# Up projection of a streaming encoder step: state stores issued by GpSimd, filters nine steps behind, another order of the first group's blocks

## The chip, the cores and the metric

The kernel runs on one core of a Trainium2 chip, and its time is the device time in microseconds of one execution. The engines named here are TensorE (PE; its weight loads are shown as PEld), VectorE (DVE), ScalarE (ACT), GpSimd (POOL) and SyncE (SP). DMAs are issued from the queues of SP, ACT and POOL.

## The reference

One layer of a hybrid encoder for 256 frames of a new stream and 16 new frames of each of 8 running streams, 384 rows in all, in float32. What matters here is the feed-forward part at the end:

```python
h2 = rmsnorm(x, norm_ffn_g)
up = h2 @ w_up                                   # (384, 2048) @ (2048, 11264)
g_half, u_half = up[..., :D_FF], up[..., D_FF:]  # D_FF = 5632
ext_f = concatenate([ffn_buf, g_half], axis=1)   # the state: the last 2 rows before
gc = causal_dwconv(ext_f, ffn_dw_w, ffn_dw_b)    # 3 taps along time
x = x + (silu(gc) * u_half) @ w_down
new_ffn = ext_f[:, -2:]                          # the state that is stored
```

Ahead of it come the norm and one combined input projection, a conformer convolution branch, forgetting attention, and the projections that join them.

## The kernel before

**Products in three parts.** A float32 product is made of three matmuls on rounded parts. Each operand is split into a high half (`hi`, a cast on ScalarE, L155) and a low half (`lo`, a subtraction on VectorE, L156), and hi*hi, hi*lo and lo*hi are added up in one PSUM bank (L1158 to L1160 in the up projection, L305 to L307 in the others).

**Weights.** They come in tiles of 256 rows x 512 columns (512 KB, `raw`, L138), issued from SP. In the feed-forward part five buffers rotate for `raw` and three for each of `hi` and `lo`. `plan` is the list of the weight tiles in the order of their use; `ahead` fetches and splits them ahead of the matmuls, with a raised priority (SPLIT_AHEAD).

**Order of the work.** TensorE's order is the program's. On the other engines, and in the queues, a planner orders the instructions at build time by priority and by its own estimate of when each can start; buffers are handed out there too. Each engine then runs its list strictly in that order. `high_priority(offset=...)` moves an instruction ahead of others in the planner's list.

**The up projection.** The 5632 columns of each half are done in 11 groups of 512 (`up_group`). In `FFN_PLAN` group 0 is followed by group 1, and then two groups alternate with one down projection: 0, 1, 2, down(0, 1), 3, 4, down(2, 3), ... 9, 10, down(8, 9, 10). So groups 2, 4, 6, 8 and 10 follow another group at once, and 3, 5, 7 and 9 follow a down projection. The 2048 rows of K are four panels of 512 (`q` = 0 to 3). Panels 0 and 1 (`MIXED`) use a fast 2x2 scheme (steps `b22`, `t3`, `t1` for the u half, `b11`, `t2`, `b21`, `t4` for the g half) that saves products by adding weight tiles on VectorE first: L200 and L205 (steps t3 and t1) and L209 (steps t2 and t4, into `sums`). Panels 2 and 3 (`PLAIN`) are done plainly, in two K blocks each: `pu0`, `pu1` for the u half and `pg0`, `pg1` for the g half. A group has 92 products of three matmuls: 4 in each of b22, t3, b11 and b21, 2 in each of t1, t2 and t4, 6 in each plain step. `phases` gives the order of the steps: in all groups but the first the plain steps are spread between the others; in the first group (`first`) they stand behind the others of the same half, so that the plain operand `xg` of panel 3, which is made last (L1050 and L1051), is wanted late. `run` walks through one half, and is called twice a group.

**Banks and evacuations.** There are five PSUM banks `acc` and three `misc`. The u half uses five `acc` banks (p5, p7, q3, q2, tu), the g half p1, tg and q6 in `misc` and p2 and q4 in `acc`. Evacuations: p5 L1195 and L1196, p7 L1199, q3 L1202, q2 L1205, the samples' rows L1208, p1 L1211 and L1212, q6 L1216 and L1219, p2 L1223, q4 L1226. Most go into row tiles u and g of the pool `block`, which has four buffers. In the first group this pool also holds the transpose of the old FFN state (L1076 to L1080).

**From rows to columns.** The rows of u and of g are transposed in 32x32 blocks on VectorE (L319), written to DRAM by four DMAs of GpSimd's queue (`turn`, L324) and read back by a fifth (L329), which completes the transpose.

**The filter.** `up_g_done` stores the state rows of a group (L1098 once, L1100 twice, 4 KB and 16 KB each) and queues the convolution with `after(n, fn)`: `fn` is emitted n + 1 steps of the `tick` counter later, a step being three products (nine matmuls). `fill` copies the columns into `extf` (ScalarE L1107; GpSimd L1110 to L1114 for the rows that overlap), `taps(m)` makes the three taps and the SiLU (L1127 to L1130), `product(m)` multiplies by u and splits the result for the down projection (L1135 to L1139), for m = 0 to 3.

Of the kernel before, what the change touches and what calls it, by code (L numbers as in the profile page):

```python
# [11 lines left out]
ALU = mybir.AluOpType  # L12
# [22 lines left out]
MIXED = (0, 1)  # L35
# [6 lines left out]
def hybrid_step(  # L42
# [121 lines left out]
    def planned(w, k0, cols, nk, *more):  # L164
        for k in range(k0, k0 + nk, 2):
            for cl in (cols,) + more:
                plan.append([rows_of(w, k, c, n) for c, n in cl])
# [3 lines left out]

    def phases(first):
        def spread(steps, plain):
            if first:
                return steps + plain
            n, m = len(steps), len(plain)
            out = []
            for i, st in enumerate(steps):
                out.append(st)
                out += plain[i * m // n:(i + 1) * m // n]  # L180
            return out

        up = [(what, q) for q in MIXED for what in ("b22", "t3", "t1")]
        gate = [(what, q) for q in MIXED for what in ("b11", "t2")] + [(what, q) for q in MIXED for what in ("b21", "t4")]
        return [spread(up, [(f"pu{h}", q) for q in PLAIN for h in range(2)]),
                spread(gate, [(f"pg{h}", q) for q in PLAIN for h in range(2)])]

    def planned_mixed(w, c1, c2, first):
        held = {}

        def add(fn):
            plan.append(lambda: split(fn(), 512))
# [15 lines left out]
        def grown(q, name):  # L208
# [5 lines left out]
                "b21": lambda q: single("b21", 4 * q + 2, c1), "t4": lambda q: grown(q, "b21")}  # L214
        for steps in phases(first):
            for what, q in steps:
                if what[0] == "p":
                    planned(w, 4 * q + 2 * int(what[2]), [({"u": c2, "g": c1}[what[1]], 512)], 2)
                else:
                    add(lambda what=what, q=q: make[what](q))  # L220

# [34 lines left out]
    def after(units, fn):  # L256
        later.append([units, fn])
# [836 lines left out]
    def up_g_done(g, box):  # L1094
        def done():
            cs = slice(512 * g, 512 * (g + 1))
            rows = box[0].rows
            nc.sync.dma_start(prompt_ffn[0, 0, :, cs], rows[126:128, 1, :])  # L1098
            for r in range(2):
                nc.sync.dma_start(sample_ffn[0, :, r, cs], rows[14 + r::16, 2, :])  # L1100
            gd = box[0].moved().rearrange("p i t q c -> p (i t) q c")

            def fill():
                for m in range(4):
# [9 lines left out]
                    nc.gpsimd.tensor_copy(e5[:, 0, 1, 0, 0:2], e5[:, 3, 0, 1, 16:18])  # L1114
            after(7, fill)

# [15 lines left out]
            def product(m):  # L1132
# [6 lines left out]
                tt(lo, av, f(hi), op=ALU.subtract)  # L1139
            pace = 1 if g == 10 else 2  # L1140
            for m in range(4):
                after(8 + pace * m, lambda m=m: taps(m))
                after(9 + pace * m + pace, lambda m=m: product(m))
        return done
# [24 lines left out]
    def up_group(g):  # L1169
# [34 lines left out]
        def q2(ps):  # L1204
            stt(rows("u")[:, 1], ps, scale[1], e1, op0=ALU.mult, op1=ALU.subtract)  # L1205

# [23 lines left out]

        def products(steps):
            return [plain(q, int(what[2]), *({"u": ("q3", "q2", "tu"), "g": ("p2", "q4", "tg")}[what[1]]))
                    if what[0] == "p" else pairs(q, *made[what]) for what, q in steps]

        up, gate = phases(g == 0)
        run(products(up), forms, dict(p5=out(p5), p7=out(p7), q3=out(q3), q2=out(q2), tu=sample("u")))
        tt(rows("u")[:, 1], rows("u")[:, 1], rows("g")[:, 1], op=ALU.subtract)
        run(products(gate), forms, dict(p1=out(p1), q6=q6, p2=out(p2), q4=out(q4), tg=sample("g")))
        up_g_done(g, [Turned(block, rows("g"))])()

# [81 lines left out]
```

## Time and profile before

| | us |
|---|---|
| median of 3 runs | 2006.79 (2005.66 to 2010.06) |
| the profiled execution | 2007.59 |
| its span in the trace | 2005.8 |
| TensorE, VectorE, ScalarE, GpSimd busy | 1970.9, 1268.0, 893.0, 237.6 |
| feed-forward part in the trace | from 913.6 to the end |

Matmuls are pipelined: one of 512 columns is shown with 0.39 us, though the next may start 0.23 us after it. A row of the timeline gives start, duration, engine, line, operation, tiles, and in brackets how long the engine had been idle and what ended that. A row of the windows gives, for one stretch, its length and the busy time of each engine with the number of instructions, the granted share of TensorE's clock, the share of the DMA engines and GB/s. "SPq" and "POOLq" are the queues' own instructions.

### The profile page before, as it was taken

The numbers are of one execution on the slowest core, as the hardware profiler recorded it, in microseconds if no ns is written. First come the engines' busy times: TensorE is split into PE (matmuls) and PEld (weight loads), VectorE is DVE, ScalarE is ACT, GpSimd is POOL, SyncE is SP. The second block draws the span as 40 slices with busy tenths as digits, with TensorE's granted clock in tenths as the row PEclk, the third lists the DMA queues.
The fourth block names the chain that finished last, engine by engine and source line by source line (L and its number), as shares of the span: only waits on it lengthen the run. The fifth ranks groups of instructions, "written<-read, shape, count | busy, mean of one in ns | idle before, by whom it ended". The sixth has DMA issues, their size and how long they took to land.

```text
span 2005.8 us, 24829 instructions
## 1 busy us (share of the span) xinstructions
PE 1970.9 (98%) x9254; PEld 1652.0 (82%) x9254; DVE 1268.0 (63%) x1692; ACT 893.0 (45%) x1308; POOL 237.6 (12%) x494
## 2 busy tenths in 40 slices
PE   9999999999999999999999999899999999999999
PEld 9999878888888888887777888788778877887787
DVE  4478889647556346547688647754775577556853
ACT  5433354554335323445465534543454445443541
POOL 1001121100000002011121200220011012101110
PEclk9999999999999999999999999999999999999999
DMA  6555776664444458566755775476557655776563
GB/s 182 160 168 159 227 235 209 203 180 139 124 129 124 131 166 277 197 229 197 231 161 181 214 204 166 158 217 198 168 182 219 188 177 166 216 210 189 176 203 115
DMA packets 200224, 369.74 MB, mean 184 GB/s; under 512 B 16078, under 2 KB 66249, under 8 KB 200095
## 3 DMA queue, kind: packets, MB, share of 16 engines
q1 hardware_dynamic: 179159, 284.72, 45.7%
q0 software_dynamic: 20624, 83.29, 14.7%
q8 instruction: 72, 1.18, 0.2%
q14 instruction: 49, 0.40, 0.1%
q10 hardware_dynamic: 320, 0.14, 0.0%
HBM read 313.32 MB, written 55.24 MB: 184 GB/s over the span
## 4 chain that ended last, share of the span: by engine, by line
PE 76%; DVE 11%; DMA 9%; issue 3%; ACT 1%; POOL 0%; DVEq 0%; SPq 0%; POOLq 0%
PE acc L305 16%; PE acc L306 16%; PE acc L307 16%; DMA raw<-in_w_up_dram 7%; DVE lo L156 5%; PE acc L1159 4%; PE acc L1160 4%; PE acc L1158 4%; DVE ut L570 2%; PE misc L1160 2%; PE misc L1158 2%; PE misc L1159 2%; PE acc L302 2%; PE acc L300 2%; PE acc L301 2%
## 5 line engine op out<-in xcount | busy, mean ns | idle before, releaser
L155 ACT CAST hi<-raw 128x1024 fp32r<-128x1024 f32 (+2 forms) x481 | 497.5, 1035 | 867.6 <-PE acc L307 465.5
L156 DVE TENSOR_TENSOR lo<-raw,hi 128x1024 fp32r<-128x1024 f32 (+2 forms) x481 | 576.8, 1203 | 461.2 <-ACT hi L155 460.0
L305 PE MATMUL acc<-hi,hT 128*128 128x512 f32 (+1 forms) x704 | 270.8, 385 | 0.1
L306 PE MATMUL acc<-lo,hT 128*128 128x512 f32 (+1 forms) x704 | 266.4, 378 | 1.0 <-DVE lo L156 1.0
L307 PE MATMUL acc<-hi,hT 128*128 128x512 f32 (+1 forms) x704 | 266.0, 378 | 0.0
L1159 PE MATMUL acc<-lo,xg 128*128 128x512 f32 x440 | 176.1, 400 | 19.8 <-DVE lo L156 19.7
L305 PE MATMUL acc<-hi,act 128*128 128x512 f32 x484 | 188.6, 390 | 0.0
L306 PE MATMUL acc<-lo,act 128*128 128x512 f32 x484 | 188.5, 390 | 0.0
L307 PE MATMUL acc<-hi,act 128*128 128x512 f32 x484 | 188.5, 390 | 0.0
L1158 PE MATMUL acc<-hi,xg 128*128 128x512 f32 x440 | 173.6, 395 | 2.6 <-ACT xg L1050 2.6
L1160 PE MATMUL acc<-hi,xg 128*128 128x512 f32 x440 | 173.6, 394 | 0.0
L306 PEld LDWEIGHTS acc<-lo,hT 128*128 128x128 f32 x704 | 132.4, 188 | 25.0 <-DVE lo L156 4.0
L570 DVE SCALAR_TENSOR_TENSOR ut<-ext,cw,ut 128x384 f32<-128x384 f32 x240 | 149.5, 623 | 5.5
L305 PEld LDWEIGHTS acc<-hi,hT 128*128 128x128 f32 x704 | 132.3, 188 | 24.1 <-issue 1.8
L307 PEld LDWEIGHTS acc<-hi,hT 128*128 128x128 f32 x704 | 132.2, 188 | 22.7
L324 POOL DMA_DIRECT2D turn<-block x124 | 68.3, 558 | 616.7 <-DVE block L319 612.6
L1159 PEld LDWEIGHTS acc<-lo,xg 128*128 128x128 f32 x440 | 83.8, 190 | 46.4 <-DVE lo L156 29.4
L1159 PE MATMUL acc<-lo,xm 128*128 128x512 f32 x308 | 120.6, 391 | 1.3 <-DVE lo L156 1.3
L1158 PE MATMUL acc<-hi,xm 128*128 128x512 f32 x308 | 120.1, 390 | 1.7 <-ACT block L1199 1.7
L1160 PE MATMUL acc<-hi,xm 128*128 128x512 f32 x308 | 120.0, 390 | 0.0
L307 PEld LDWEIGHTS acc<-hi,act 128*128 128x128 f32 x484 | 90.9, 188 | 18.9
L305 PEld LDWEIGHTS acc<-hi,act 128*128 128x128 f32 x484 | 90.9, 188 | 18.8
(348 smaller groups left out, 3413.4 us busy)
## 6 DMA issues: line engine op xcount, KB each, us to landing
raw<-in_w_up_dram SPq DMA_DIRECT2D x198, 512.0 KB
raw<-in_w_in_dram SPq DMA_DIRECT2D x96, 512.0 KB
raw<-in_w_down_dram SPq DMA_DIRECT2D x88, 512.0 KB
turn<-block POOLq DMA_DIRECT2D x120, 192.0 KB, 5.1
block<-turn POOLq DMA_DIRECT2D x30, 768.0 KB, 6.2
raw<-in_w_in_dram SPq DMA_DIRECT2D x64, 256.0 KB
raw<-in_w_out_dram SPq DMA_DIRECT2D x32, 512.0 KB
y_rows<-part POOLq DMA_DIRECT2D x16, 768.0 KB, 6.7
```

The costliest lines, as they stand in the source:

```text
L155: nc.scalar.copy(hi[:, k, :o], raw[:, k, :o])
L156: tt(lo[:, k, :o], raw[:, k, :o], f(hi[:, k, :o]), op=ALU.subtract)
L300: mm(o, hi[:, kk, s], ah, start=st, stop=False)
L301: mm(o, hi[:, kk, s], al, start=False, stop=False)
L305: mm(o, ah[:, s], hi[:, kk, :n], start=st, stop=False)
L306: mm(o, ah[:, s], lo[:, kk, :n], start=False, stop=False)
L307: mm(o, al[:, s], hi[:, kk, :n], start=False, stop=sp)
L324: nc.gpsimd.dma_start(d[:, :, i, :].rearrange("j r n -> r j n"), src[32 * i:32 * i + 32, :].rearrange("r (j n) -> r j n", j=4))
L570: stt(o, v, wc, o, op0=ALU.mult, op1=ALU.add)
L1158: mm(o, ah, hi[:, kk, :], start=st, stop=False)
L1159: mm(o, ah, lo[:, kk, :], start=False, stop=False)
L1160: mm(o, al, hi[:, kk, :], start=False, stop=last[b] == (i, n))
```

## The change

- The three state stores of each group are issued from GpSimd's queue instead of SP's.
- `fill`, `taps` and `product` of groups 0 to 9 are queued two steps later: fill 9 steps behind the group instead of 7, the taps from 10 and the products from 13 on. Group 10 keeps 7, 8 and 10.
- In the first group the two K blocks of panel 3 of the u half (`pu[-2:]`) come behind b11 and t2 of panel 0, and at its end the plain steps of the g half stand between the steps b21 and t4 instead of behind them. The other groups keep their order.
- Both halves of a group are one sequence (`steps`) and one call of `run`. The subtraction of g's second row tile from u's (L1237) is issued right behind q2's evacuation instead of between the two calls.

```diff
--- before.py
+++ after.py
@@ -169,21 +169,18 @@
     sums, new_sum = {}, []
     PLAIN = [q for q in range(4) if q not in MIXED]
 
-    def phases(first):
-        def spread(steps, plain):
-            if first:
-                return steps + plain
-            n, m = len(steps), len(plain)
-            out = []
-            for i, st in enumerate(steps):
-                out.append(st)
-                out += plain[i * m // n:(i + 1) * m // n]
-            return out
+    def steps(first):
+        def spread(heavy, plain):
+            n, m = len(heavy), len(plain)
+            return [x for i in range(n) for x in [heavy[i]] + plain[i * m // n:(i + 1) * m // n]]
 
         up = [(what, q) for q in MIXED for what in ("b22", "t3", "t1")]
-        gate = [(what, q) for q in MIXED for what in ("b11", "t2")] + [(what, q) for q in MIXED for what in ("b21", "t4")]
-        return [spread(up, [(f"pu{h}", q) for q in PLAIN for h in range(2)]),
-                spread(gate, [(f"pg{h}", q) for q in PLAIN for h in range(2)])]
+        top = [(what, q) for q in MIXED for what in ("b11", "t2")]
+        low = [(what, q) for q in MIXED for what in ("b21", "t4")]
+        pu, pg = ([(f"p{side}{h}", q) for q in PLAIN for h in range(2)] for side in "ug")
+        if first:
+            return up + pu[:-2] + top[:-2] + pu[-2:] + top[-2:] + spread(low, pg)
+        return spread(up, pu) + spread(top + low, pg)
 
     def planned_mixed(w, c1, c2, first):
         held = {}
@@ -212,12 +209,11 @@
         make = {"b22": lambda q: single("b22", 4 * q + 2, c2), "t3": both, "t1": top,
                 "b11": lambda q: single("b11", 4 * q, c1), "t2": lambda q: grown(q, "b11"),
                 "b21": lambda q: single("b21", 4 * q + 2, c1), "t4": lambda q: grown(q, "b21")}
-        for steps in phases(first):
-            for what, q in steps:
-                if what[0] == "p":
-                    planned(w, 4 * q + 2 * int(what[2]), [({"u": c2, "g": c1}[what[1]], 512)], 2)
-                else:
-                    add(lambda what=what, q=q: make[what](q))
+        for what, q in steps(first):
+            if what[0] == "p":
+                planned(w, 4 * q + 2 * int(what[2]), [({"u": c2, "g": c1}[what[1]], 512)], 2)
+            else:
+                add(lambda what=what, q=q: make[what](q))
 
     V_COLS = [[(O_V + 344 * i, 344)] for i in range(3)]
     K_COLS = [[(O_K + 512 * i, 512)] for i in range(2)]
@@ -1095,9 +1091,9 @@
         def done():
             cs = slice(512 * g, 512 * (g + 1))
             rows = box[0].rows
-            nc.sync.dma_start(prompt_ffn[0, 0, :, cs], rows[126:128, 1, :])
+            nc.gpsimd.dma_start(prompt_ffn[0, 0, :, cs], rows[126:128, 1, :])
             for r in range(2):
-                nc.sync.dma_start(sample_ffn[0, :, r, cs], rows[14 + r::16, 2, :])
+                nc.gpsimd.dma_start(sample_ffn[0, :, r, cs], rows[14 + r::16, 2, :])
             gd = box[0].moved().rearrange("p i t q c -> p (i t) q c")
 
             def fill():
@@ -1112,7 +1108,8 @@
                     nc.gpsimd.tensor_copy(e5[:, :, 0:2, 1, 0:2], e5[:, :, 0:2, 0, 16:18])
                     nc.gpsimd.tensor_copy(e5[:, 1:4, 0:2, 0, 0:2], e5[:, 0:3, 0:2, 1, 16:18])
                     nc.gpsimd.tensor_copy(e5[:, 0, 1, 0, 0:2], e5[:, 3, 0, 1, 16:18])
-            after(7, fill)
+            lag, pace = (7, 1) if g == 10 else (9, 2)
+            after(lag, fill)
 
             gcs = gates[g] = [p_f.tile([P, NT], F32, tag="gc", bufs=4, name="gc") for _ in range(4)]
             act = acts[g] = gp.tile([P, 2, 4, NT], F32R, tag=f"G{1 + g % 3}", name=f"act{g}")
@@ -1137,10 +1134,9 @@
                 hi, lo = natural(act[:, 0, m, :]), natural(act[:, 1, m, :])
                 nc.scalar.copy(hi, av)
                 tt(lo, av, f(hi), op=ALU.subtract)
-            pace = 1 if g == 10 else 2
             for m in range(4):
-                after(8 + pace * m, lambda m=m: taps(m))
-                after(9 + pace * m + pace, lambda m=m: product(m))
+                after(lag + 1 + pace * m, lambda m=m: taps(m))
+                after(lag + 2 + pace * m + pace, lambda m=m: product(m))
         return done
 
     spent = [0]
@@ -1202,7 +1198,10 @@
             stt(rows("u")[:, 0], ps, scale[0], e0, op0=ALU.mult, op1=ALU.subtract)
 
         def q2(ps):
-            stt(rows("u")[:, 1], ps, scale[1], e1, op0=ALU.mult, op1=ALU.subtract)
+            u = rows("u")[:, 1]
+            with tc.high_priority(offset=FFN_AHEAD):
+                stt(u, ps, scale[1], e1, op0=ALU.mult, op1=ALU.subtract)
+            tt(u, u, rows("g")[:, 1], op=ALU.subtract)
 
         def sample(name):
             return out(lambda ps: nc.scalar.activation(rows(name)[:, 2], ps, AF.Identity, scale=scale[2]))
@@ -1228,14 +1227,10 @@
         made = {"b22": (("q3", 2), ("tu", 4)), "t3": (("p7", 3), ("tu", 8)), "t1": (("p5", 0),),
                 "b11": (("p1", 5), ("tg", 8)), "t2": (("q6", 1),), "b21": (("tg", 9), ("p2", 6)), "t4": (("q4", 7),)}
 
-        def products(steps):
-            return [plain(q, int(what[2]), *({"u": ("q3", "q2", "tu"), "g": ("p2", "q4", "tg")}[what[1]]))
-                    if what[0] == "p" else pairs(q, *made[what]) for what, q in steps]
-
-        up, gate = phases(g == 0)
-        run(products(up), forms, dict(p5=out(p5), p7=out(p7), q3=out(q3), q2=out(q2), tu=sample("u")))
-        tt(rows("u")[:, 1], rows("u")[:, 1], rows("g")[:, 1], op=ALU.subtract)
-        run(products(gate), forms, dict(p1=out(p1), q6=q6, p2=out(p2), q4=out(q4), tg=sample("g")))
+        seq = [plain(q, int(what[2]), *({"u": ("q3", "q2", "tu"), "g": ("p2", "q4", "tg")}[what[1]]))
+               if what[0] == "p" else pairs(q, *made[what]) for what, q in steps(g == 0)]
+        run(seq, forms, dict(p5=out(p5), p7=out(p7), q3=out(q3), q2=q2, tu=sample("u"),
+                             p1=out(p1), q6=q6, p2=out(p2), q4=out(q4), tg=sample("g")))
         up_g_done(g, [Turned(block, rows("g"))])()
 
     def down_jobs(gs, last):
```

## The prediction

> **What bounds the kernel now.** First the page's busy times and the waits of TensorE (engine and line that wait, what ended the wait, us in total, times, longest):
>
> ```profile
> PE 1970.9 (98%) x9254; PEld 1652.0 (82%) x9254; DVE 1268.0 (63%) x1692; ACT 893.0 (45%) x1308; POOL 237.6 (12%) x494
> ...
> PE acc L1159 <- DVE lo L156: 21.0, 23, 4.7
> PE acc L1158 <- ACT xg L1050: 2.6, 1, 2.6
> PE acc L1158 <- ACT block L1199: 1.7, 1, 1.7
> ```
>
> TensorE is busy nearly throughout, so the change can win only idle pieces, and those lie in the feed-forward part: 25.3 us in three kinds. Next the windows over single groups of the up projection; each computes the same 276 matmuls.
>
> ```profile
> core 0: us, PE busy (x) PEld busy (x) DVE busy (x) ACT busy (x) POOL busy (x), PEclk, DMA share, GB/s
> 983.48:1048.13 64.65, 63.44 (x278) 51.60 (x277) 53.08 (x63) 35.79 (x46) 13.11 (x26) 1.00 0.60 180
> 1180.50:1243.67 63.17, 62.85 (x278) 51.75 (x277) 42.74 (x42) 27.45 (x30) 3.66 (x6) 1.00 0.58 172
> 1243.67:1314.26 70.59, 65.39 (x279) 52.97 (x278) 50.30 (x60) 34.56 (x45) 14.44 (x26) 0.98 0.55 174
> 1442.42:1509.43 67.01, 63.96 (x278) 51.40 (x277) 50.23 (x60) 34.36 (x45) 10.99 (x26) 1.00 0.58 182
> 1638.19:1706.92 68.73, 65.46 (x279) 52.81 (x278) 50.26 (x60) 34.47 (x45) 14.48 (x26) 0.98 0.56 178
> ```
>
> A group that follows a down projection (1180.50) takes 63.2 us, 0.23 us a matmul. One that follows another group at once (group 4 at 1243.67, 6 at 1442.42, 8 at 1638.19) carries that group's filter too, 50 us of VectorE instead of 43, and loses 7.4, 3.8 and 5.6 us. Group 1 (983.48) loses only 1.5. What those losses are, the timeline of group 4 shows: start, duration, engine, line, tile, idle time and its end.
>
> ```profile
> 1258.96 1.05 ACT L155 CAST hi<-raw 128x1024 fp32r<-128x1024 f32 x1 [3.03 <-PE acc L1160]
> ...
> 1259.34 1.22 DVE L156 TENSOR_TENSOR lo<-sums,hi 128x1024 fp32r<-128x1024 f32 x1
> 1267.53 1.23 DVE L209 TENSOR_TENSOR sums<-sums,raw 128x1024 f32<-128x1024 f32 x1 [6.98 <-DMA raw<-in_w_up_dram]
> 1268.67 2.35 DVE L156 TENSOR_TENSOR lo<-raw,hi 128x1024 fp32r<-128x1024 f32 x2
> ...
> 1269.95 0.50 PE L1159 MATMUL acc<-lo,xg 128*128 128x512 f32 x1 [4.73 <-DVE lo L156]
> ```
>
> The high half was ready at 1260.0. Its low half stood on VectorE behind an addition (L209) for a later step, which waited 6.98 us for its weights. So the limit is the order on VectorE together with late loads; no engine is full over the group.
>
> **The change part by part.** *The first group's last plain K block.* Before, plain block 3 (xg of panel 3) follows block 2 at once:
>
> ```profile
> 938.49 0.91 ACT L1050 CAST xg<-block 128x384 fp32r<-128x384 f32 x2
> ...
> 940.86 1.03 DVE L1051 TENSOR_TENSOR xg<-block,xg 128x384 fp32r<-128x384 f32 x2 [0.81 <-ACT xg L1050]
> ...
> 939.04 0.59 PE L1158 MATMUL acc<-hi,xg 128*128 128x512 f32 x1 [2.56 <-ACT xg L1050]
> ...
> 939.30:942.70 3.40, 3.40 (x9) 2.55 (x9) 1.77 (x4) 1.94 (x5) 0.00 (x0) 0.50 1.00 181
> 942.80:946.20 3.40, 3.40 (x16) 2.80 (x15) 0.07 (x1) 1.05 (x1) 0.00 (x0) 1.00 0.20 65
> ```
>
> The matmul waits 2.56 us, and then the granted clock is 0.50 for 3.4 us: 9 matmuls where the next 3.4 us hold 15 or 16, six or seven fewer at 0.23 us, 1.5 us. After the change b11 and t2 of mixed block 0 come in between: 6 products, 18 matmuls, 4.1 us. TensorE reaches block 3 at 939.04 - 2.56 + 4.1 = 940.6, when the split that released it (938.49 + about 0.5) is 1.5 us old; the second half is wanted at 944.7, and its low halves end at 941.9. The whole 4.1 us (2.6 + 1.5) goes; at least 2.6, if some other wait draws the clock down. [...]
>
> *What is late next there* is a PSUM bank:
>
> ```profile
> 946.13 1.23 DVE L156 TENSOR_TENSOR lo<-sums,hi 128x1024 fp32r<-128x1024 f32 x1 [4.25 <-ACT hi L155]
> ...
> 948.53 1.64 DVE L319 STREAM_TRANSPOSE block<-block 128x1408 f32<-128x1408 f32 x1
> ...
> 957.54 0.56 POOL L329 DMA_DIRECT2D block<-turn  x1 [4.89 <-DMA turn<-block]
> ...
> 959.52 0.74 DVE L1202 SCALAR_TENSOR_TENSOR block<-acc,r,sums 128x512 f32<-128x512 f32 x1
> ...
> 961.70 0.50 PE L1158 MATMUL acc<-hi,xm 128*128 128x512 f32 x1 [1.72 <-ACT block L1199]
> ```
>
> The evacuations of the up sums (L1199, L1202) need block buffers that the FFN state's transpose holds (948.53) until its turn DMAs have landed (957.54). q4 needs its bank at the same place of the order as before, so TensorE would arrive 4.1 us earlier. Does the state chain move too? Its transpose stood behind a low split that had waited 4.25 us for ScalarE's high split, and that follows TensorE. I take it to move along: the 1.72 us stay. Bounds: all of it gone (-1.7) to a chain that stays put (+4.1).
>
> *The first group's end* is plain steps only before (four of them, 16 us with one load each), and low and plain steps in turn after, as in other groups. That quiet end let group 1 start with its loads ahead: it lost 1.5 us, the next lowest 3.8. I take +1.0 of the 2.3 between them, since the new end is still easier than other groups' (one plain step after every heavy one); bounds 0 and +2.3.
>
> *The stores.* Three an up group, from SP's queue to GpSimd's:
>
> ```profile
> 1240.90 0.37 SPq L138 DMA_DIRECT2D raw<-in_w_up_dram  x1
> 1244.08 0.28 SPq L1098 DMA_DIRECT2D out_dram<-block  x1
> 1244.70 1.21 SPq L1100 DMA_DIRECT2D out_dram<-block  x2
> 1249.28 2.70 SPq L138 DMA_DIRECT2D raw<-in_w_up_dram  x2
> ...
> 1250.76 2.18 POOL L324 DMA_DIRECT2D turn<-block  x4 [11.38 <-DVE block L319]
> ...
> L324 POOL DMA_DIRECT2D turn<-block x124: 551/553/599, 740.0 to 1907.3; - x124
> ```
>
> SP waits for the group's evacuations from 1241.3 to 1245.9 and looks blocked. But the next load starts only at 1249.28, 3.4 us after the last store, for a raw buffer still in use. Taking 0.28 + 1.21 us off SP brings no load forward: 0. On GpSimd three issues cost 3 x 0.55 = 1.7 us (0.60 at most: 1.8). They find it idle: 11.38 us before the turn DMAs, of which 6.1 lie after the last store's data (1244.7 to 1250.8). So 0; without that cover turn, landing and fill come 1.7 us later, less than the fill's own delay below. Behind the stores queue only this group's turn DMAs and, in the last group, the loads of y for the last down projection.
>
> [...]
>
> *Filters nine steps behind.* A step is nine matmuls, 2.05 us; fill, taps and products of groups 0 to 9 come 4.1 us later in the order. The last group keeps its lag of 7.
>
> ```profile
> ACT extf L1107 <- DMA block<-turn: 7.8, 5, 2.7
> ...
> 1466.42 0.94 ACT L1107 COPY extf<-block 128x384 f32<-128x384 f32 x2 [2.59 <-DMA block<-turn]
> ...
> 1473.09 1.03 ACT L155 CAST hi<-raw 128x1024 fp32r<-128x1024 f32 x1
> ...
> 1475.44 0.50 PE L1159 MATMUL misc<-lo,xm 128*128 128x512 f32 x1 [0.73 <-DVE lo L156]
> 1481.12 0.50 PE L1159 MATMUL acc<-lo,xg 128*128 128x512 f32 x1 [1.30 <-DVE lo L156]
> ...
> 1281.00:1289.50 8.50, 8.35 (x37) 6.62 (x36) 8.50 (x11) 4.84 (x7) 1.03 (x1) 1.00 0.49 133
> 1289.50:1297.70 8.20, 8.20 (x38) 6.80 (x37) 8.20 (x12) 5.35 (x8) 0.00 (x0) 1.00 0.43 140
> ...
> L1129 DVE SCALAR_TENSOR_TENSOR gc<-extf,fw,gc 128x384 f32<-128x384 f32 x88 | 51.8, 614 | 5.9 <-ACT gc L1127 5.8
> L1139 DVE TENSOR_TENSOR act<-gc,act 128x384 fp32r<-128x384 f32 x44 | 23.9, 554 | 3.6 <-ACT act L1138 3.4
> ```
>
> Five fills hold up ScalarE for the block's landing, 7.8 us in all and 2.7 at most; 4.1 us later all five find it landed. In group 4 that wait was not on the path (the high split above was long ready): 0. In group 6 the fill pushed taps and then the high split at 1473.09: I credit the 0.73 us at 1475.44 and half of the 1.30 at 1481.12 (the up sums' evacuations stand there too), -1.3 with bounds 0 and -2.0. What it costs: VectorE is full from 1281 to 1297.7 (8.50 of 8.50, 8.20 of 8.20), and filter work slides further into that stretch. As splits and evacuations have priority in the planner, I take it that the filter yields: 0. Upper bound: one filter pair, two taps at 0.61 and a product's two operations at 0.55 (the row of the second), 2.3 us, ahead of a wanted low split in each of five second groups: +11.7.
>
> *One sequence; q2's subtraction behind its evacuation*: the same instructions in nearly the same place, 0; if that subtraction steps in front of a low split it belongs to the bound just given.
>
> **Sum.** -4.1 + 0 + 1.0 + 0 - 1.3 + 0 = -4.4 us. The profiled execution took 2007.59 us (span 2005.8): 2003.2. It lies 0.8 above the median of 2006.79, so 2002.4.
>
> **Rivals.**
> 1. *The bank takes the gain back.* The state chain hangs on its own loads and landings, not on TensorE; then the wait at 961.70 grows by 4.1 us. For it: 4.89 us of the chain are a landing. Against: its transpose followed a wait for ScalarE. 2002.4 + 4.1 = 2006.5.
> 2. *A better order on VectorE.* The planner orders everything anew; groups 6 and 10 already run without group 4's long wait. If the additions no longer stand ahead of ready low splits, group 4's 4.73 + 1.5 (clock 0.98 in its window) and most of group 8's excess over group 6 (1.7) and its own lesser waits go, some 10 us: 1992. Against: no edit names that order.
> 3. *Slower: filter work ahead of low splits* where VectorE is full, 2.3 us in each second group. It decides from two groups on (4.4 / 2.3); three give +2.5 over before, 2009.3, and all five 2014.1.
> 4. *The stores do bring loads forward* (what the queue change would be for): against it stand the 3.4 us above; I fold its chance into rival 2.
>
> **How the numbers follow.** About 0.2% (4 us) is what a measurement of this kernel can tell from no change. Forecast 0.42, its own range 2000.4 to 2004.4, a little over half of it faster by more than 4 us (below 2002.8): 0.25 faster, 0.17 same. Rival 1: 0.17, same. Rivals 2 and 4: 0.24, faster. Rival 3: 0.17, slower. Faster 0.49, same 0.34, slower 0.17. The range 1992 to 2010 leaves out the far ends of rivals 2 and 3, under 0.2.
>
> **What the profile after would show.** Right: no wait on xg (L1050) and no half clock near 939; a wait of some 1.7 us on L1199; no ScalarE wait of L1107 on the block's landing; SP's loads at the same distance from VectorE's splits though no store stands between; group 1 at 65 to 66 us. Wrong: a wait of 4 us or more on L1199 (rival 1); second groups at 64 us (rival 2), or at 70 with taps or products right before the low split that TensorE waits for (rival 3).

## The result, and the profile after

The changed kernel takes 2016.19 us in the median, the kernel before 2009.21 us in the same set of runs (2006.79 in the three shown at first). The ratio is 1.0033, with a 95% interval from 1.0019 to 1.0047: slower by 0.33%, some 6.6 us, where 4.4 us of gain were forecast. One of the changed kernel's eight executions took 5105.91 us; it counts in the median and not in the ratio. The profiled execution took 2013.98 us with a span of 2012.3, 6.5 above the span before. Lines 1050, 1107, 1129, 1158 to 1160, 1199, 200, 205, 209, 324 and 329 of the kernel before are now 1046, 1103, 1126, 1154 to 1156, 1195, 197, 202, 206, 320 and 325; the subtraction is L1204.

The waits of TensorE in the feed-forward part of the kernel after (waiting engine, tile and line, what ended the wait, us in total, times, longest):

```profile
PE acc L1155 <- DVE lo L156: 24.1, 28, 2.7
PE misc L1155 <- DVE lo L156: 5.7, 3, 4.2
PE acc L1154 <- ACT block L1195: 1.0, 1, 1.0
PE acc L1156 <- DVE xg L1047: 0.6, 1, 0.6
PE acc L1154 <- ACT xg L1046: 0.2, 1, 0.2
```

The wait on xg is gone: 2.6 us before, 0.2 and 0.6 now. The bank wait (L1195) is 1.0 where it was 1.7. What grew is the wait on low splits: 21.0 us on acc before, 29.8 on acc and misc now. The windows say where. First the kernel before, groups 0 and 1, then the kernel after: groups 0 and 1, the former place of the half clock, and a new one.

```profile
913.70:983.59 69.89, 65.05 (x277) 52.67 (x276) 49.05 (x58) 34.34 (x45) 11.58 (x20) 0.98 0.70 214
983.59:1048.24 64.65, 63.44 (x277) 51.60 (x276) 53.19 (x63) 35.79 (x46) 13.11 (x26) 1.00 0.60 181
```

```profile
912.40:985.87 73.47, 66.85 (x277) 53.12 (x276) 49.89 (x60) 34.45 (x45) 10.74 (x21) 0.95 0.67 207
985.87:1053.58 67.71, 64.34 (x277) 51.33 (x276) 52.14 (x62) 36.02 (x46) 13.04 (x28) 1.00 0.57 174
939.90:943.30 3.40, 2.81 (x11) 2.00 (x12) 3.29 (x5) 3.37 (x7) 0.00 (x0) 1.00 0.75 234
969.60:976.40 6.80, 5.12 (x12) 4.07 (x13) 3.90 (x4) 0.02 (x1) 2.19 (x4) 0.50 0.69 188
```

Group 0 takes 3.6 us more and group 1 3.1 more; from group 2's start to group 10's it is 787.4 us before and 788.9 after. So the groups in which the filters lie barely moved, and the loss stands in the first two. Near 940 the clock is whole now. Near 970 it is 0.50, and here is why, in the timeline of VectorE and of TensorE after:

```profile
958.85 0.74 DVE L1203 SCALAR_TENSOR_TENSOR block<-acc,r,sums 128x512 f32<-128x512 f32 x1
963.90 1.23 DVE L197 TENSOR_TENSOR sums<-raw 128x1024 f32<-128x1024 f32 x1 [4.30 <-DMA raw<-in_w_up_dram]
965.04 0.69 DVE L1215 TENSOR_TENSOR sums<-misc,sums 128x512 f32<-128x512 f32 x1
965.64 0.69 DVE L1204 TENSOR_TENSOR block<-block 128x512 f32<-128x512 f32 x1
966.24 1.41 DVE L1218 SCALAR_TENSOR_TENSOR block<-sums,r,block 128x512 f32<-128x512 f32 x2
967.57 0.75 DVE L1218 SCALAR_TENSOR_TENSOR block<-sums,nr,block 128x512 f32<-128x512 f32 x1
968.23 1.89 DVE L315 STREAM_TRANSPOSE block<-block 128x512 f32<-128x512 f32 x3
970.04 2.32 DVE L156 TENSOR_TENSOR lo<-raw,hi 128x1024 fp32r<-128x1024 f32 x2
...
971.28 0.80 PE L1155 MATMUL misc<-lo,xm 128*128 128x512 f32 x1 [4.22 <-DVE lo L156]
```

TensorE stands at the third low step of group 0 (b21 of panel 1; the expectations below call it the first) and wants the low split that starts at 970.04. On VectorE that split stands behind group 1's first addition (L197), which waited 4.30 us for its weights, and then behind eight operations, q6's evacuation, the subtraction and the transposes, 965.04 to 970.04. In the kernel before, the four low steps came in a row behind the top ones. Their last split (961.09) was through before q6's evacuation began (962.73), and the splits of plain steps then took turns with it:

```profile
961.09 1.23 DVE L156 TENSOR_TENSOR lo<-sums,hi 128x1024 fp32r<-128x1024 f32 x1 [0.17 <-ACT hi L155]
962.73 0.69 DVE L1216 TENSOR_TENSOR sums<-misc,sums 128x512 f32<-128x512 f32 x1 [0.42 <-ACT sums L1211]
963.34 0.68 DVE L1237 TENSOR_TENSOR block<-block 128x512 f32<-128x512 f32 x1
964.52 1.23 DVE L156 TENSOR_TENSOR lo<-raw,hi 128x1024 fp32r<-128x1024 f32 x1 [0.50 <-ACT hi L155]
965.66 1.41 DVE L1219 SCALAR_TENSOR_TENSOR block<-sums,r,block 128x512 f32<-128x512 f32 x2
967.25 2.54 DVE L156 TENSOR_TENSOR lo<-raw,hi 128x1024 fp32r<-128x1024 f32 x2 [0.18 <-ACT hi L155]
```

The idle 4.22 us were followed by 12 matmuls at up to twice their length, 2.5 us more: 6.7 us in all at one step, twice what xg gave back.

### The profile page after: what moved, and what is told of

Same layout as the page of the kernel before. It is cut to its first block, busy times and chain, and to the rows that moved or that the text cites. A ratio compares the mean times of both kernels' runs of the same rounds, so it can differ in the third digit from the quotient of the medians.

```text
span 2012.3 us, 24838 instructions
## 1 busy us (share of the span) xinstructions
PE 1972.1 (98%) x9254; PEld 1649.8 (82%) x9254; DVE 1267.4 (63%) x1692; ACT 893.4 (44%) x1308; POOL 261.0 (13%) x527
## 4 chain that ended last, share of the span: by engine, by line
PE 76%; DVE 10%; DMA 9%; issue 3%; ACT 1%; POOL 1%; DVEq 0%; SPq 0%; POOLq 0%
PE acc L301 17%; PE acc L302 17%; PE acc L303 17%; DMA raw<-in_w_up_dram 7%; DVE lo L156 5%; PE acc L1155 4%; PE acc L1156 4%; PE acc L1154 4%; PE misc L1156 2%; PE misc L1155 2%; PE misc L1154 2%; PE acc L298 2%; PE acc L296 1%; PE acc L297 1%; DVE ut L566 1%
```

## The experiments

Differences are ratios of the runs to those of the kernel before, with 95% intervals, and in us as that share of 2009. The last two columns are of the profiled execution: the time from a group's first matmul to the next group's. The kernel before was run again beside each set (medians from 2008.1 to 2010.6), so medians of different sets are not to be subtracted. Single profiles scatter too: with five buffers and the old first order (before, e1, e4 to e7, e12) group 0 takes 68.0 to 70.3 us, though its steps are the same.

| Kernel | median us | ratio to before | us | group 0 | group 1 |
|---|---|---|---|---|---|
| before | 2009 | 1 | 0 | 69.9 | 64.7 |
| after | 2016.19 | 1.0033 [1.0019, 1.0047] | +6.6 | 73.5 | 67.7 |
| e1 after, old first order | 2021.69 | 1.0052 [1.0038, 1.0066] | +10.4 | 70.3 | 71.7 |
| e2 new first order, one sequence | 2019.11 | 1.0039 [1.0025, 1.0053] | +7.8 | 73.2 | 70.9 |
| e3 after, plain end of group 0 | 2017.81 | 1.0035 [1.0021, 1.0048] | +7.0 | 68.5 | 71.7 |
| e4 one sequence | 2010.00 | 0.9995 [0.9984, 1.0006] | -1.0 | 68.0 | 64.0 |
| e5 stores | 2017.18 | 1.0056 [1.0037, 1.0075] | +11.3 | 69.3 | 66.8 |
| e6 filters nine behind | 2007.20 | 0.9993 [0.9980, 1.0006] | -1.4 | 68.3 | 64.9 |
| e7 wait on GpSimd | 2010.35 | 1.0016 [1.0002, 1.0031] | +3.2 | 69.8 | 69.2 |
| e8 later K block, plain end | 2016.55 | 1.0040 [1.0024, 1.0056] | +8.0 | 68.8 | 72.7 |
| e9 seven buffers at first | 2010.25 | 0.9989 [0.9979, 0.9999] | -2.2 | 72.4 | 62.6 |
| e10 e8 with them | 2014.35 | 1.0017 [1.0008, 1.0025] | +3.4 | 75.7 | 62.6 |
| e11 e5 with them | 2008.90 | 0.9996 [0.9981, 1.0010] | -0.8 | 68.4 | 62.7 |
| e12 stores, GpSimd in order | 2012.54 | 1.0007 [0.9994, 1.0020] | +1.4 | 69.9 | 64.2 |
| e13 seven buffers throughout | 1980.24 | 0.9862 [0.9846, 0.9878] | -27.7 | 71.2 | 62.6 |
| e14 after, with them | 1994.64 | 0.9936 [0.9923, 0.9950] | -12.9 | 76.0 | 62.6 |
| e15 e2 with them | 1986.62 | 0.9892 [0.9874, 0.9910] | -21.7 | 76.7 | 62.6 |
| e16 e8 with them | 1983.22 | 0.9874 [0.9858, 0.9890] | -25.3 | 75.0 | 62.6 |
| e17 e5 with them | 1987.08 | 0.9898 [0.9882, 0.9914] | -20.5 | 70.0 | 62.6 |
| e18 e6 with them | 1977.24 | 0.9844 [0.9828, 0.9860] | -31.3 | 68.1 | 62.6 |

### Which part costs (e1 to e6, e8)

The first theory (A) was drawn from the trace above: the mixed end of group 0 costs, the later plain K block gains, the rest is nothing. e1 takes the first group's order back:

```
-            return up + pu[:-2] + top[:-2] + pu[-2:] + top[-2:] + spread(low, pg)
+            return up + pu + top + low + pg
```

> The changed kernel with one edit taken back: the first up group goes in its old order again (heavy up steps, all plain up steps, top, low, plain gate steps); stores on GpSimd, filters nine steps behind and the one sequence stay. Theory A (the 6.6 us lost come from the first group's new end, where low steps and plain gate steps alternate: 6.75 us at the first low step and about 3 us in group 1, less about 4 us won at the group's top steps): the time comes back to that of the kernel before, within 2 us, with the 2.6 us wait on xg and the half clock behind it back, and no idle time of more than 1 us at the first low step. Theories B (filters nine behind cost), C (stores on GpSimd cost) and D (one sequence, VectorE's moved subtraction, costs): the loss stays, 5 to 8 us above the kernel before.

e2 is the change with `nc.sync` for the stores and `lag, pace = (7, 1) if g == 10 else (7, 2)`:

> The changed kernel with the stores back on SyncE and the filters seven steps behind: what is left is the first group's new order and the one sequence. Theory A: slower than the kernel before by 5 to 8 us, as the whole change is, with the same idle time of about 4 us ahead of the first low step of the first group, behind VectorE's addition that waits for a raw load. Theories B and C: back to the kernel before or 2 to 4 us below it, since xg's wait is gone.

e3 ends the first group with plain steps:

```
-            return up + pu[:-2] + top[:-2] + pu[-2:] + top[-2:] + spread(low, pg)
+            return up + pu[:-2] + top[:-2] + pu[-2:] + top[-2:] + low + pg
```

> The changed kernel, but the first group ends with plain gate steps alone again (low steps first, then all plain gate steps); the last plain K block of the up half still stands behind the first top steps, and stores, filters and the one sequence are those of the change. Theory A: the 6.75 us at the first low step and the 3 us in group 1 go, the gain at xg stays: 2 to 5 us below the kernel before. If the later plain K block itself is what costs (theory A2), it stays 5 us or more above the kernel before. B, C, D: it stays slower than the kernel before by 3 us or more.

e4 is the edits of e1 and e2 together:

> Only the one sequence of steps is left of the change (VectorE's subtraction moved from between the two halves to behind each evacuation of a plain up step); old first order, stores on SyncE, filters seven behind. Theory A: within 2 us of the kernel before. Theory D: slower by 3 us or more.

Theory A fell by half. e2 came out as it said (+7.8 us, the same wait of 4.1 us at the same step), and e4 leaves theory D nothing. But e1 did not come back, so the stores or the filters cost too; and e3 did not gain, by these or by the later K block, which it cannot tell apart. So each was put alone on the kernel before: e5 `nc.sync` to `nc.gpsimd` in the three stores, e6 `after(9, fill)` with taps and products two steps later, and e8, the first order of e3 with stores on SyncE and a lag of seven.

> The kernel before with the up state stores moved to GpSimd and nothing else. Theory S (the three stores of a group wait in GpSimd's order for the last evacuation and hold up the read-back of the first turned block behind them, by 3.5 us in the run with the old first order; the read-back then moves its 768 KB beside the next group's raw loads, which land 11 us after their issue, not 6.6): slower than the kernel before by 6 to 13 us, the loss in groups 1 and 2 first. Theory L (the filters nine steps behind are what costs): within 2 us of the kernel before.

> The kernel before with the filters nine steps behind instead of seven and nothing else. Theory S: within 3 us of the kernel before. Theory L: slower by 6 to 13 us, since taps and products then stand among later low splits on VectorE.

> Only the first group's new order, but with an end of plain gate steps as before (low steps, then all plain gate steps); the last plain K block of the up half stands behind the first top steps; stores on SyncE, filters seven behind. Theory A (the mixed end costs, the later plain K block gains): 2 to 5 us below the kernel before, with no idle time over 2 us at a low step of group 0 and group 1 under 3 us of idle time. Theory A2 (the later plain K block brings group 1's additions behind their loads): not faster than the kernel before, with 3 us or more lost in group 1.

The stores alone cost 11.3 us, the filters nothing that can be told from zero, and the later K block 8.0 us with no mixed end (theory A2). The mixed end on top of it adds nothing to that (e2, 7.8); in the profiles e2 takes 4.4 us more than e8 in group 0 and 1.8 less in group 1. Two separate losses, then, of which the change as a whole shows only 6.6 us: what the new first order costs by itself.

### The stores (e5, e7, e12)

GpSimd's timeline around the first stores, before and in e5:

```profile
976.61 2.18 POOL L324 DMA_DIRECT2D turn<-block  x4 [9.35 <-DVE block L319]
984.58 0.56 POOL L329 DMA_DIRECT2D block<-turn  x1 [5.79 <-DMA turn<-block]
991.24 1.10 POOL L324 DMA_DIRECT2D turn<-block  x2 [6.10 <-DVE block L319]
```

```profile
975.31 2.18 POOL L324 DMA_DIRECT2D turn<-block  x4 [9.56 <-DVE block L319]
985.39 0.53 POOL L1098 DMA_DIRECT2D out_dram<-block  x1 [7.90 <-DVE block L1226]
985.91 1.15 POOL L1100 DMA_DIRECT2D out_dram<-block  x2
987.05 0.55 POOL L329 DMA_DIRECT2D block<-turn  x1
```

L329 reads the turned up sums back, 768 KB. Before, it went out 8.0 us after the first of its turn DMAs, when they had landed; in e5 after 11.7, because the stores stand in front of it and wait for the group's last evacuation (L1226). The read-back then falls beside the loads that group 1 needs: five go out within 11.5 us from 986.26 on (before within 9.4 from 988.03 on), and the additions at L205 and L209 wait 4.72 and 3.77 us for theirs, before 2.62 and 4.53. In GpSimd's order the stores stand ahead of it in groups 0 to 2 of e5, and behind it from group 3 on. But only in group 0 does that delay it: in groups 1 and 2 it goes out 8.4 and 8.0 us after the first turn DMA, before 8.7 and 9.0. e7 brings the wait without stores (the first edit below, with `scr` a small new tile); e12 brings the stores on GpSimd without that place (the second edit):

```
-            rows = box[0].rows
+            rows = box[0].rows; nc.gpsimd.tensor_copy(scr[:], rows[96:128, 1, 0:2])
...
-    wide[0] = True
+    wide[0] = True; pool_order = tc.manual_schedule(engines={ENG.Pool}); pool_order.__enter__()
```

> The kernel before, stores on SyncE as they were; added is one copy of 32x2 elements on GpSimd in each group that reads the last evacuated block, into a tile that nothing reads. It stands where the stores stood in GpSimd's order, ahead of the read-back of the first turned block, and so brings the same wait without any store. Theory S (the wait ahead of the read-back costs): the read-back is issued about 3 us later and the time is 5 us or more above the kernel before, most of what the stores cost. Theory Q (the stores' own small packets beside the raw loads, or their issue on GpSimd, cost): within 2 us of the kernel before.

> Stores on GpSimd, and nothing else of the change, but GpSimd's instructions go in the order in which the program emits them in the up and down part: the read-back of the first turned block then stands ahead of the stores, and does not wait for the last evacuation. Theory S (the place ahead of the read-back is what the stores cost): within 3 us of the kernel before. Theory Q (stores issued by GpSimd cost by themselves, wherever they stand): slower by 6 us or more.

```profile
982.10 0.56 POOL L329 DMA_DIRECT2D block<-turn  x1 [5.62 <-ACT block L1208]
984.81 0.53 POOL L1098 DMA_DIRECT2D out_dram<-block  x1 [2.16 <-DVE block L1226]
985.33 1.13 POOL L1100 DMA_DIRECT2D out_dram<-block  x2
```

e7 is the clean one: in its trace all 1692 instructions of VectorE and all 1308 of ScalarE stand in the order of the kernel before. Group 0's read-back goes out 11.3 us after the first turn DMA (986.41 - 975.08) instead of 8.0, group 1 waits 4.4 us for low splits instead of 1.2, and the kernel loses 3.2 us (0.4 to 6.2), less than the 5 expected. So the wait on GpSimd is shown to cost that, by way of the late read-back. The other 8 us of e5 are not explained by it. They come with another order on VectorE (134 of its 1692 places differ, the first at 987.9 of the trace before), and in the profile they are scattered: against the kernel before e5 loses 2.1 us in group 1, 2.5 from group 2's start to group 3's and 3.9 from group 8's to group 9's, the last two with no late read-back of their own.

With the read-back ahead of the stores (982.10 in e12) the stores cost 1.4 us, nothing that can be told from zero, where theory Q expected 6 or more. That speaks for the place in the queue, but e12 puts all of GpSimd in another order and changes VectorE's too, and no run has that order with the stores on SyncE. A gain of the order that hides a cost of the stores is not excluded.

### The later K block, and raw buffers (e8 to e11)

VectorE in e8, and SyncE's loads (a row gives the first start and the time to the end of the last):

```profile
957.98 1.22 DVE L156 TENSOR_TENSOR lo<-sums,hi 128x1024 fp32r<-128x1024 f32 x1 [1.49 <-ACT hi L155]
959.13 0.74 DVE L1198 SCALAR_TENSOR_TENSOR block<-acc,r,sums 128x512 f32<-128x512 f32 x1
...
963.69 0.74 DVE L1218 SCALAR_TENSOR_TENSOR block<-sums,nr,block 128x512 f32<-128x512 f32 x1
964.35 1.22 DVE L156 TENSOR_TENSOR lo<-raw,hi 128x1024 fp32r<-128x1024 f32 x1
...
956.52 9.44 SPq L138 DMA_DIRECT2D raw<-in_w_up_dram  x2
```

With plain block 3 between the top steps, the up sums' evacuation comes only two top steps ahead of q6's, and the planner joins them: eight operations, 959.13 to 964.35, and no low split among them. A low split is what sets a raw buffer free, so SyncE issues one load at 956.52 and the next 9.1 us later; before, five went out within 13.6 us from 956.58 on. Group 1's additions then wait 20.5 us for the loads, before 12.3, and group 1 takes 72.7 us. If that is the way of the loss, more raw buffers must take it away. e9 to e11 use two panels that lie unused in the first up groups:

```
-        if wide[0] and n % 5 > 2:
-            raw = p_sg.tile([P, 2, 512], F32, tag=f"S{n % 5 - 3}", name="raw")
+        if wide[0]: wide.append(n)
+        if wide[0] and (k := ((n - wide[1]) % 7 if n - wide[1] < 42 else n % 5)) > 2:
+            raw = p_sg.tile([P, 2, 512], F32, tag=f"S{k - 3}", name="raw")
```

> The kernel before, but the loads of the first 42 chunks from the first up group on go round seven raw buffers (two more panels that lie unused there) instead of five. A base for the next two; nothing else is changed. Theory R (in the up groups VectorE's additions wait for raw loads that could not be issued sooner because no buffer was free): 0 to 5 us below the kernel before, the idle time in groups 0 to 2 smaller. If the loads are held by something else: within 1 us of the kernel before.

> The first group's later plain K block (with an end of plain gate steps, stores on SyncE, filters seven behind; with five buffers it was 7.8 us slower than the kernel before) with the same seven raw buffers. Theory R (the loss is that the evacuations of both halves stand in one row on VectorE, 5.2 us without a low split, so that no raw buffer comes free for 9.1 us and group 1's additions wait for their loads): the loss shrinks to 3 us or less against the kernel with seven buffers and the old order, and group 1 loses under 5 us. Rival P (the order of the steps itself, by what TensorE and VectorE do, costs): 6 us or more above it still, with the same idle time in group 1.

> The kernel before with the stores on GpSimd (with five buffers 8 to 11 us slower than the kernel before) and the seven raw buffers in the first groups. Theory R: the loss in groups 1 and 2 (5 us of it in the profile) shrinks by half or more, that of the later groups (five buffers there) stays: 3 to 7 us above the kernel with seven buffers and stores on SyncE. If the loss comes from the transfers' own throughput (the read-back beside the loads): groups 1 and 2 lose as much as with five buffers.

Group 1 loses nothing any more in any of them: 62.6 us is 276 matmuls at 0.227. The stores' loss is gone in the sum (e11 stands 1.4 us above e9, inside their intervals, where 3 to 7 were expected). In the profiles that is partly luck: from group 2's start to group 10's e11 takes 795.2 us, as e5 does (794.6), against 787.9 in e9, and makes up for it in group 0, ahead of every store (68.4 against 72.4), and behind group 10's start (166.8 against 170.5). What the buffers are shown to take away is the loss in group 1. e10 still stands 5.6 us above e9, in the profiles 3.3 of it in group 0: theory R holds for group 1, and for group 0 it is open. There the small state loads go out 27.1 us after the group's start (942.8 - 915.7) and in e9 after 21.4 (936.3 - 914.9), so e10 does not show the order alone; for the next runs the two extra buffers set in behind the state loads.

### Seven buffers in all up groups (e13 to e18)

```
+        k = n % (7 if 223 < n < 266 or n > 285 and 5 < (n - 286) % 52 < 32 else 5)
+        if wide[0] and k > 2: raw = p_sg.tile([P, 2, 512], F32, tag=f"S{k - 3}", name="raw")
```

> The kernel before with seven raw buffers instead of five in all up groups, from the eighth wide chunk of group 0 on (so that the small state loads keep their place) and, behind a down stage, from the seventh chunk on. Theory R (VectorE's additions wait for loads that no free buffer let out): groups 1 to 10 lose less than half of the 33 us that they lose with five buffers: 10 to 20 us below the kernel before. If the loads are held by the transfers' throughput: within 3 us of it.

> The whole change with the same seven raw buffers. Theory R (both losing parts, the first group's order and the stores on GpSimd, cost only by way of raw loads that come late): within 3 us of the kernel with seven buffers and without the change, on either side. Rival P (order and stores cost by themselves): 5 to 8 us above it, as with five buffers.

> The first group's new order as in the change (mixed end), stores on SyncE, filters seven behind, with the same seven raw buffers. Theory R: the addition of group 1 ahead of group 0's low split no longer waits 4 us for its load, and the 4 us won at xg stay: 1 to 5 us below the kernel with seven buffers and the old order. Rival P: 5 us or more above it.

> The later plain K block with an end of plain gate steps, stores on SyncE, filters seven behind, with the same seven raw buffers. Theory R: 1 to 5 us below the kernel with seven buffers and the old order. Rival P (the row of evacuations on VectorE costs by itself): 4 us or more above it, lost in group 0.

e13 gains 27.7 us, more than expected. VectorE's and TensorE's waits from group 1 to group 10, before and in e13:

```profile
DVE sums L209 <- DMA raw<-in_w_up_dram: 61.1, 26, 7.0
DVE raw L205 <- DMA raw<-in_w_up_dram: 58.5, 18, 4.5
DVE sums L200 <- DMA raw<-in_w_up_dram: 28.6, 14, 4.7
...
PE acc L1159 <- DVE lo L156: 20.5, 22, 4.7
```

```profile
DVE sums L209 <- DMA raw<-in_w_up_dram: 37.8, 14, 3.8
DVE sums L200 <- DMA raw<-in_w_up_dram: 20.3, 12, 4.0
DVE raw L205 <- DMA raw<-in_w_up_dram: 13.5, 8, 3.6
...
PE acc L1159 <- DVE lo L156: 1.6, 4, 0.7
```

The additions' waits for loads fall from 148.2 to 71.6 us, and TensorE's wait behind them from 20.5 to 1.6. That was the bound of the groups. On this base the order does not gain either: e15 stands 6.0 us above e13 (executions of 1985.6 to 1987.3 against 1979.2 to 1981.6), and e16 2.4, with intervals that overlap; in the profiles both lose in group 0 (76.7 and 75.0 against 71.2). In e15 the low split stands in the same row as in the kernel after, with another addition in front:

```profile
968.12 1.22 DVE L202 TENSOR_TENSOR raw<-raw 128x1024 f32<-128x1024 f32 x1 [3.95 <-DMA raw<-in_w_up_dram]
...
972.45 1.89 DVE L315 STREAM_TRANSPOSE block<-block 128x512 f32<-128x512 f32 x3
974.27 1.18 DVE L156 TENSOR_TENSOR lo<-raw,hi 128x1024 fp32r<-128x1024 f32 x1
...
975.51 0.80 PE L1155 MATMUL misc<-lo,xm 128*128 128x512 f32 x1 [5.45 <-DVE lo L156]
```

By its number e15 falls to rival P, but it does not separate the two. The addition still waits 3.95 us for its load, and that load went out at 962.88, when the low split of 961.63 had set its buffer free: group 0 is still short of buffers with seven. Without that wait some 1.5 of the 5.45 us would be left, an estimate from these rows. e16's 2.4 us fall to neither theory. So for group 0 it stays open how much the order on VectorE costs where no load is late. e14 stands 14.9 us above e13, 6.0 of it the order as in e15. For the rest, stores and filters alone:

> Seven raw buffers in all up groups, and of the change only the stores on GpSimd. Theory R (with five buffers the stores cost only by raw loads that come late): within 3 us of the kernel with seven buffers alone. Theory S2 (they also hold GpSimd's order up where the fill needs the read-back, as before the last up group, where the copy into the filter's tile waited 8.2 us in the whole change on seven buffers): 4 to 9 us above it, in the groups that carry a filter.

> Seven raw buffers in all up groups, and of the change only the filters nine steps behind. Theories R and S2: within 2 us of the kernel with seven buffers alone. Theory L (the later filter takes VectorE's and ScalarE's time from the splits of the next group's later steps): 4 to 9 us above it.

The stores again, 7.2 us above e13 (S2). The filters nine behind are 3.6 us better, with intervals that overlap a little; but 3.1 of the 5.0 us between the two profiles lie in group 0, ahead of the first filter, where VectorE's order is the same in both. There the clock after the xg wait was 0.54 in e13 and 1.00 in e18. So the gain is not shown to be the filters'. In e17 and e14 the last read-back stands on GpSimd behind a load of y that waits 11.5 and 11.9 us for a panel which a raw load still holds, and the fill waits 6.7 and 8.2 us at the longest for its landing; e13 has the read-back ahead of that load. This accounts for group 10 (from its start to the end 172.0 and 173.7 us against 167.9); the other microseconds are spread, and where they come from was not tried. e18 is the fastest kernel of the study: 1977.24 us, 0.9844 of the kernel before [0.9828, 0.9860], and 1.9% below the kernel after. Its waits of TensorE in the feed-forward part:

```profile
PE acc L1158 <- ACT xg L1050: 2.6, 1, 2.6
PE acc L1158 <- ACT block L1199: 1.7, 1, 1.7
PE acc L307 <- DVE act L1139: 0.5, 2, 0.3
PE acc L1159 <- DVE lo L156: 0.4, 1, 0.4
```

The xg wait that the change set out from is now the largest that is left.

## Why the prediction was wrong, by its steps

- **xg and the half clock (-4.1).** Right in its wait, by luck in its clock. The waits there are 0.2 and 0.6 us and the clock is 1.00; some 3.3 us were won between these two profiles, the second half of xg being 0.6 late. But the 1.5 us of half clock do not belong to the wait: in e4, e6, e11 and e18 the same wait of 2.56 us is followed by a whole clock (see the end). Where the clock stays whole, only the wait is there to be won.
- **The bank (0, bounds -1.7 to +4.1).** Right: 1.04 us against 1.72. Rival 1 did not come.
- **The first group's new order (-4.1 + 0 + 1.0).** This is the step that failed. Alone it was to win 3.1 us, and e2, which has it without stores and filters, loses 7.8; e4 and e6 clear the rest of the change but the stores. Two terms had it wrong.
  - **The first group's end (+1.0, bounds 0 to +2.3).** The wait at b21 and the clock behind it took 6.7 us of group 0, and group 1 lost 3.1. The bounds were taken from what other groups lose as a whole. The mechanism stood in the prediction, in the timeline of group 4: a ready split behind an addition that waits. It was not asked of the new order which addition and which evacuations would stand in front of the low split that now comes earlier. How much the mixed end costs by itself was not run; on top of the later K block it adds nothing (e2 against e8).
  - **The later plain K block itself.** No term of the sum had a cost for it. With the stores where they were, e8 shows that it brings two evacuations together, holds the loads back 9.1 us, and costs 8.0 us even with a plain end.
- **Stores (0).** Wrong alone: 11.3 us in e5. The idle time of GpSimd was read in group 4, where the read-back stands ahead of the stores. "Behind the stores queue only this group's turn DMAs" is false in groups 0 to 2 of e5. Of the 11.3 us, some 3.2 are shown to come from the wait on GpSimd (e7); the rest is open. In the change itself the mixed end makes the planner put group 0's read-back ahead of the stores (it is issued at 978.73, the stores from 986.43 on), and only groups 1 and 2 have it behind. That, and a group 1 that is slowed by either cause and not by both in turn, may be why the two losses do not add; this is argued, not shown. As forecast, the issues by themselves are cheap: the 33 of the kernel after took 0.52 to 0.60 us each.
- **Filters (-1.3).** Nothing to be measured (e6). The claim that all fills would find their block landed was wrong: 7.9 us of such waits after, 7.8 before. They were not on the path.
- **One sequence (0).** Right (e4).
- **Rivals.** The kernel became slower by neither way that was named for it: rival 3 (filter work ahead of low splits) is refuted by e6, whose interval ends at +0.06%. Rival 4 is refuted by e5, where the first load that stood behind the stores before goes out 0.9 us earlier, counted from group 0's start (986.26 - 912.78 against 988.03 - 913.70), and the kernel is slower.

## What to carry to other kernels

When steps are moved, ask at the new place which instructions the in-order engine will have ahead of the operand that is wanted, and above all whether one of them waits for a transfer; the worth of the wait removed says nothing of that. Here a wait of 2.6 us was removed, and one of 4.2 us put in its place. Before a DMA issue goes to an "idle" queue, look in each stage, not in one, at what is issued behind it and whether the moved issue waits for something late. And where additions wait for loads all along, count the buffers first: two unused panels were worth 28 us here, while with five buffers no part of the change moved more than 12, and none of them down by more than its noise. And compare the granted clock before a gain of 2 us is put down to an edit.

## What the runs showed of the hardware

Here the time that TensorE stood idle does not by itself tell whether the clock is halved behind it. The wait on xg is 2.56 us in twelve of the profiles. In eight of them (before, e1, e5, e7, e10, e12, e13, e17) the granted clock over the 3.4 us behind it is 0.50 to 0.63, in four (e4, e6, e11, e18) it is 1.00:

```profile
938.42 0.50 PE L1154 MATMUL acc<-hi,xg 128*128 128x512 f32 x1 [2.56 <-ACT xg L1046]
938.72:942.12 3.40, 3.40 (x16) 2.57 (x15) 1.74 (x4) 1.91 (x5) 0.00 (x0) 1.00 1.07 169
```

These two rows are e4's: 16 matmuls where the kernel before has 9. Group 0 is shorter in just these four (68.0 to 68.4 us) than in the seven of the other eight that have the old first order (69.3 to 71.2; e10 has the later K block). A wait of 1.65 us with one of 0.58 behind it was followed by 0.57 in e15 and by 1.00 in e14, and one of 3.47 us by 1.00 (e4, at 1662.28). After 4.22 us the clock was 0.50 in the kernel after, for some 5 us (12 matmuls from 971.28 on). What decides was not tried.
